# Max-pool and subtract: tiles of six rows in four buffers, without ScalarE and in program order

## The chip, the cores and the metric

The kernel runs on one core of one Trainium2 chip. The metric is the device time of one execution in microseconds (us), given as the median of several runs; less is better.

## The reference

```python
def reference(x):                      # x: (8, 64, 256, 256) float32
    x_r = x.reshape(B, C, oH, 8, oW, 8)
    pooled = x_r.max(axis=(3, 5))
    upsampled = np.repeat(np.repeat(pooled, 8, axis=2), 8, axis=3)
    return (x - upsampled).astype(np.float32)
```

Each 8 x 8 window of each image is reduced to its maximum, and that maximum is subtracted from every element of the window. The input has 134.2 MB and the output as much; every element is read once and written once.

## The kernel before

Eight image lines of 256 floats, which hold 32 whole windows side by side, make one "row" of 2048 floats (8 KB). There are 16384 rows. A tile has 128 partitions with R = 2 consecutive rows in each, so 16 KB per partition and 2 MB in all, and the loop runs over 64 tiles. For each tile:

- L42: SP (SyncE) issues the load of the tile into `dat`, from a pool of 8 buffers.
- L49: VectorE takes the maximum over each window of one row, seen as (32 windows, 8 lines, 8 columns), into `pooled` (32 values). One instruction per row, two per tile.
- L56: ScalarE copies `pooled` into `rep`, each value eight times in a row, so that `rep` has a full line of 256 values for each row. One ACTIVATE per tile, for both rows.
- L64: VectorE subtracts `rep` from `dat` in place; the line of `rep` is read again for each of the eight lines. One instruction per row.
- L74: ScalarE's queue issues the store of `dat` to the output.

The order on each engine isn't the order of the program text: a scheduler places the instructions. On VectorE it has grouped them, three to five reduces of several tiles and then four to six subtracts, and on ScalarE's queue it has put up to three ACTIVATEs ahead of the stores. A load into a buffer waits until the store that last used the buffer has landed. All loads go through SP's queue in order, all stores through ScalarE's queue in order; both queues are served by the same 16 DMA engines.

Of the kernel before, what the change touches and what calls it, by code (L numbers as in the profile page):

```python
# [1 line left out]

# [4 lines left out]


@with_exitstack  # L10
def kernel(
    ctx: ExitStack,
    tc: tile.TileContext,
    x: bass.AP,
    out: bass.AP,
):
    nc = tc.nc
    P = nc.NUM_PARTITIONS

    B, C, H, W = x.shape  # L20
    pH = pW = 8
    oH, oW = H // pH, W // pW

    x_rows = x.rearrange("b c (oh ph) w -> (b c oh) (ph w)", ph=pH)
    out_rows = out.rearrange("b c (oh ph) w -> (b c oh) (ph w)", ph=pH)
    n_rows = x_rows.shape[0]
    row_len = x_rows.shape[1]

    R = 2
    rows_per_tile = P * R  # L30
    ntiles = n_rows // rows_per_tile
    assert n_rows % rows_per_tile == 0

    data_pool = ctx.enter_context(tc.tile_pool(name="data_pool", bufs=8))
    small_pool = ctx.enter_context(tc.tile_pool(name="small_pool", bufs=4))

    for i in range(ntiles):
        dat = data_pool.tile([P, R, row_len], mybir.dt.float32, name="dat")
        src = x_rows[i * rows_per_tile : (i + 1) * rows_per_tile].rearrange(
            "(p r) d -> p (r d)", r=R  # L40
        )
        nc.sync.dma_start(out=dat.rearrange("p r d -> p (r d)"), in_=src)  # L42

        pooled = small_pool.tile([P, R, oW], mybir.dt.float32, name="pooled")
        rep = small_pool.tile([P, R, W], mybir.dt.float32, name="rep")

        for r in range(R):
            in_v = dat[:, r].rearrange("p (ph ow pw) -> p ow ph pw", ph=pH, ow=oW, pw=pW)
            nc.vector.tensor_reduce(  # L49
                out=pooled[:, r],  # L50
                in_=in_v,
                axis=mybir.AxisListType.XY,
                op=mybir.AluOpType.max,
            )

        nc.scalar.activation(  # L56
            out=rep.rearrange("p r (ow pw) -> p (r ow) pw", pw=pW),
            in_=pooled.rearrange("p r ow -> p (r ow)").to_broadcast([P, R * oW, pW]),
            func=mybir.ActivationFunctionType.Copy,
        )  # L60

        for r in range(R):
            dat_v = dat[:, r].rearrange("p (ph w) -> p ph w", ph=pH)
            nc.vector.tensor_tensor(  # L64
                out=dat_v,
                in0=dat_v,
                in1=rep[:, r].unsqueeze(1).to_broadcast([P, pH, W]),
                op=mybir.AluOpType.subtract,
            )

        dst = out_rows[i * rows_per_tile : (i + 1) * rows_per_tile].rearrange(
            "(p r) d -> p (r d)", r=R
        )
        nc.scalar.dma_start(out=dst, in_=dat.rearrange("p r d -> p (r d)"))  # L74


# [1 line left out]
_INS = ['x']  # L78
_OUTS = [((8, 64, 256, 256), 'float32')]


# [23 lines left out]
```

## Time and profile before

| | |
|---|---|
| median of 5 runs | 631.89 us (630.63 to 632.32) |
| the profiled execution: its own time | 632.32 us |
| its span, first to last instruction | 630.3 us |
| VectorE busy | 564.8 us (90%), 256 instructions |
| ScalarE busy | 39.5 us (6%) |
| data moved by the DMA engines | 268.48 MB, mean 426 GB/s |
| load, issue to landing, shortest / median | 7.8 / 30.0 us |
| store, issue to landing, shortest / median | 6.3 / 18.8 us |

A profile is taken from one execution; the span leaves out what lies before the first and after the last instruction. "Busy" of an engine is the time in which it ran instructions. An engine that is busy 90% of the span isn't yet the one that sets the time: what counts is which wait ends last in each stretch. The page cuts the span into 40 slices and gives for each the busy share of the engines in tenths, and the GB/s that the DMA engines moved. A group of instructions is shown with its busy time and the mean duration of one, then with the idle time of the engine just before them and what ended it. "Issue to landing" of a DMA is the time from its issue until its semaphore tells that all its data has arrived.

### The profile page before, as it was taken

The page shows a single profiled execution, that of the slowest core. Times are in us where ns is not written, and L with a number is a line of the kernel's source. Part 1 is how long each engine was busy: PE and PEld are TensorE (multiplying, and loading weights), DVE is VectorE, ACT ScalarE, POOL GpSimd, SP SyncE. Part 2 cuts the span into 40 slices and gives each one's busy share as a digit, 9 for nine tenths or more (in the row PEclk, how much of TensorE's full clock was granted, in tenths as well). Part 3 has the DMA queues.
Part 4 walks back from the last instruction along what each step waited for, and adds up shares of the span by engine and source line. Part 5 has one row for each costly group of instructions (what it writes and reads, how often), then busy time and mean ns, then how long its engine had stood idle before and what let it go on. Part 6 is the DMA issues. An engine that isn't in the chain of part 4 may idle for free.

```text
span 630.3 us, 730 instructions
## 1 busy us (share of the span) xinstructions
DVE 564.8 (90%) x256; ACT 39.5 (6%) x65; POOL 0.2 (0%) x4
## 2 busy tenths in 40 slices
DVE  4999999889889889889889898898998988988985
ACT  1000010010000000000001001001001001001000
POOL 0000000000000000000000000000000000000000
DMA  9999999999999999999999999999999999999997
GB/s 362 417 432 431 426 432 431 431 430 433 432 432 432 433 432 432 430 429 429 431 432 430 433 432 430 433 433 432 432 430 430 429 428 432 430 433 432 433 409 335
DMA packets 18437, 268.48 MB, mean 426 GB/s; under 512 B 2048, under 2 KB 2048, under 8 KB 2048
## 3 DMA queue, kind: packets, MB, share of 16 engines
q1 hardware_dynamic: 9216, 134.22, 50.0%
q10 hardware_dynamic: 9216, 134.22, 49.8%
q14 instruction: 5, 0.04, 0.0%
HBM read 134.22 MB, written 134.22 MB: 426 GB/s over the span
## 4 chain that ended last, share of the span: by engine, by line
DMA 83%; DVE 15%; issue 1%; DVEq 0%; ACT 0%; SPq 0%; ACTq 0%
DMA dat<-in_x_dram 50%; DMA out_dram<-dat 33%; DVE dat L64 9%; DVE pooled L49 6%; DVEq L100 0%; ACT rep L56 0%; SPq L42 0%; ACTq L74 0%; DVEq L64 0%; ACTq L56 0%
## 5 line engine op out<-in xcount | busy, mean ns | idle before, releaser
L49 DVE TENSOR_REDUCE pooled<-dat 128x32 f32<-128x2048 f32 x128 | 285.1, 2278 | 57.6 <-DMA dat<-in_x_dram 57.6
L64 DVE TENSOR_TENSOR dat<-dat,rep 128x2048 f32<-128x2048 f32 x128 | 284.0, 2284 | 0.8 <-ACT rep L56 0.8
L56 ACT ACTIVATE rep<-pooled 128x512 f32<-128x512 f32 x64 | 38.2, 624 | 578.4 <-DMA dat<-in_x_dram 408.1
L56 ACT ACT_TABLE_LOAD x1 | 1.3, 1283 | 0.7 <-PEq L89 0.7
L89 POOL MEMSET const-bfloat16-1.0<- 128x1 bf16 x1 | 0.1, 102 | 0.0
L89 POOL MEMSET const-uint8-127<- 128x1 uint8 x1 | 0.1, 102 | 0.0
L89 POOL MEMSET const-float32-0.0<- 128x1 f32 x1 | 0.1, 99 | 0.2 <-issue 0.2
L89 POOL MEMSET const-float32-1.0<- 128x1 f32 x1 | 0.1, 99 | 0.0
## 6 DMA issues: line engine op xcount, KB each, us to landing
dat<-in_x_dram SPq DMA_DIRECT2D x64, 2048.0 KB, 30.0
out_dram<-dat ACTq DMA_DIRECT2D x64, 2048.0 KB, 18.8
```

The costliest lines, as they stand in the source:

```text
L49: nc.vector.tensor_reduce(out=pooled[:, r], in_=in_v, axis=mybir.AxisListType.XY, op=mybir.AluOpType.max,)
L56: nc.scalar.activation(out=rep.rearrange("p r (ow pw) -> p (r ow) pw", pw=pW), in_=pooled.rearrange("p r ow -> p (r ow)").to_broadcast([P, ...
L64: nc.vector.tensor_tensor(out=dat_v, in0=dat_v, in1=rep[:, r].unsqueeze(1).to_broadcast([P, pH, W]), op=mybir.AluOpType.subtract,)
L89: nc = _bacc.Bacc("TRN2", target_bir_lowering=False, num_devices=1)
```

## The change

The tile has up to six rows per partition (48 KB, 6 MB in all), and there are 25 tiles of different sizes: one of two rows, twenty of six, two of two, two of one. The pool has 4 buffers, each with room for six rows, also where a tile needs fewer. One reduce takes the maxima of all rows of a tile (for a one-row tile there is a form of its own). ScalarE computes nothing and has no table to load: the subtract reads `pooled` directly, each value eight times in a row for each of the eight lines. The subtract stays one instruction per row. The scheduler is switched off with `manual_schedule`, so each engine runs its instructions in the order of the text: the reduce of a tile, its subtracts, then the next tile. Each first subtract waits on VectorE's own semaphore for the reduce ahead of it. Stores stay on ScalarE's queue, loads on SP's.

```diff
+F32 = mybir.dt.float32
+ROW = 2048
+CHUNKS = [2] + [6] * 20 + [2, 2, 1, 1]
...
-    R = 2
-    rows_per_tile = P * R
-    ntiles = n_rows // rows_per_tile
...
+    big = max(CHUNKS)
-    data_pool = ctx.enter_context(tc.tile_pool(name="data_pool", bufs=8))
-    small_pool = ctx.enter_context(tc.tile_pool(name="small_pool", bufs=4))
+    data = ctx.enter_context(tc.tile_pool(name="data", bufs=4))
+    small = ctx.enter_context(tc.tile_pool(name="small", bufs=4))
+    ctx.enter_context(tc.manual_schedule())
+    at = 0
+    for R in CHUNKS:
+        src = x_rows[at : at + P * R].rearrange("(p r) d -> p (r d)", r=R)
+        dst = out_rows[at : at + P * R].rearrange("(p r) d -> p (r d)", r=R)
+        at += P * R
+        dat = data.tile([P, big * ROW], F32, name="dat")[:, : R * ROW]
+        pooled = small.tile([P, big * oW], F32, name="pooled")[:, : R * oW]
+        nc.sync.dma_start(out=dat, in_=src)
-        for r in range(R):
-            in_v = dat[:, r].rearrange("p (ph ow pw) -> p ow ph pw", ph=pH, ow=oW, pw=pW)
+        wins = dat.rearrange("p (r ph ow pw) -> p r ph ow pw", r=R, ph=pH, ow=oW)
+        tops = pooled.rearrange("p (r ow) -> p r ow", r=R)
+        if R == 1:
             nc.vector.tensor_reduce(
-                out=pooled[:, r],
-                in_=in_v,
+                out=tops[:, 0],
+                in_=wins[:, 0].rearrange("p ph ow pw -> p ow ph pw"),
                 axis=mybir.AxisListType.XY,
                 op=mybir.AluOpType.max,
             )
-        nc.scalar.activation(
-            out=rep.rearrange("p r (ow pw) -> p (r ow) pw", pw=pW),
-            in_=pooled.rearrange("p r ow -> p (r ow)").to_broadcast([P, R * oW, pW]),
-            func=mybir.ActivationFunctionType.Copy,
-        )
+        else:
+            nc.vector.tensor_reduce(
+                out=tops,
+                in_=wins.rearrange("p r ph ow pw -> p r ow ph pw"),
+                axis=mybir.AxisListType.XY,
+                op=mybir.AluOpType.max,
+            )
         for r in range(R):
             nc.vector.tensor_tensor(
-                out=dat_v,
-                in0=dat_v,
-                in1=rep[:, r].unsqueeze(1).to_broadcast([P, pH, W]),
+                out=wins[:, r],
+                in0=wins[:, r],
+                in1=tops[:, r].unsqueeze(1).unsqueeze(3).to_broadcast([P, pH, oW, pW]),
                 op=mybir.AluOpType.subtract,
             )
-        nc.scalar.dma_start(out=dst, in_=dat.rearrange("p r d -> p (r d)"))
+        nc.scalar.dma_start(out=dst, in_=dat)
```

In the new text the load is at L44, the reduce at L56 (L49 for one row), the subtract at L63 and the store at L69.

More of the change, by code (lines that the diff above doesn't have):

```diff
@@ L21 @@
     pH = pW = 8
-    oH, oW = H // pH, W // pW
+    oW = W // pW
     x_rows = x.rearrange("b c (oh ph) w -> (b c oh) (ph w)", ph=pH)
     out_rows = out.rearrange("b c (oh ph) w -> (b c oh) (ph w)", ph=pH)
-    n_rows = x_rows.shape[0]
-    row_len = x_rows.shape[1]
-    R = 2
-    rows_per_tile = P * R
-    ntiles = n_rows // rows_per_tile
-    assert n_rows % rows_per_tile == 0
-    data_pool = ctx.enter_context(tc.tile_pool(name="data_pool", bufs=8))
-    small_pool = ctx.enter_context(tc.tile_pool(name="small_pool", bufs=4))
[L37 to L40, printed above, removed]
-        )
-        nc.sync.dma_start(out=dat.rearrange("p r d -> p (r d)"), in_=src)
-        pooled = small_pool.tile([P, R, oW], mybir.dt.float32, name="pooled")
-        rep = small_pool.tile([P, R, W], mybir.dt.float32, name="rep")
-        for r in range(R):
-            in_v = dat[:, r].rearrange("p (ph ow pw) -> p ow ph pw", ph=pH, ow=oW, pw=pW)
+    assert sum(CHUNKS) * P == x_rows.shape[0]
+    big = max(CHUNKS)
[13 more added lines that the diff above has]
+        if R == 1:
             nc.vector.tensor_reduce(
-                out=pooled[:, r],
-                in_=in_v,
+                out=tops[:, 0],
+                in_=wins[:, 0].rearrange("p ph ow pw -> p ow ph pw"),
                 axis=mybir.AxisListType.XY,
@@ L54 @@
             )
-        nc.scalar.activation(
-            out=rep.rearrange("p r (ow pw) -> p (r ow) pw", pw=pW),
-            in_=pooled.rearrange("p r ow -> p (r ow)").to_broadcast([P, R * oW, pW]),
-            func=mybir.ActivationFunctionType.Copy,
-        )
+        else:
[5 more added lines that the diff above has]
+            )
         for r in range(R):
-            dat_v = dat[:, r].rearrange("p (ph w) -> p ph w", ph=pH)
             nc.vector.tensor_tensor(
-                out=dat_v,
-                in0=dat_v,
-                in1=rep[:, r].unsqueeze(1).to_broadcast([P, pH, W]),
+                out=wins[:, r],
+                in0=wins[:, r],
+                in1=tops[:, r].unsqueeze(1).unsqueeze(3).to_broadcast([P, pH, oW, pW]),
                 op=mybir.AluOpType.subtract,
             )
[L71 to L74, printed above, removed]
+        nc.scalar.dma_start(out=dst, in_=dat)
 _INS = ['x']
```

## The prediction

> **What bounds the kernel now.** I read the page from the top: the share of each engine, then the slices, then the queues, and only then the chain, because at 90% VectorE looks like the limit and the slices say otherwise.
>
> ```profile
> DVE 564.8 (90%) x256; ACT 39.5 (6%) x65; POOL 0.2 (0%) x4
> DMA  9999999999999999999999999999999999999997
> GB/s 362 417 432 431 426 432 431 431 430 433 432 432 432 433 432 432 430 429 429 431 432 430 433 432 430 433 433 432 432 430 430 429 428 432 430 433 432 433 409 335
> q1 hardware_dynamic: 9216, 134.22, 50.0%
> q10 hardware_dynamic: 9216, 134.22, 49.8%
> L49 DVE TENSOR_REDUCE pooled<-dat 128x32 f32<-128x2048 f32 x128 | 285.1, 2278 | 57.6 <-DMA dat<-in_x_dram 57.6
> L64 DVE TENSOR_TENSOR dat<-dat,rep 128x2048 f32<-128x2048 f32 x128 | 284.0, 2284 | 0.8 <-ACT rep L56 0.8
> L56 ACT ACTIVATE rep<-pooled 128x512 f32<-128x512 f32 x64 | 38.2, 624 | 578.4 <-DMA dat<-in_x_dram 408.1
> ```
>
> The load queue (q1) and the store queue (q10) together fill 99.8% of the DMA engines' time, at 428 to 433 GB/s in nearly all slices. VectorE's 57.6 us of idle time are all waits for loads. So the transfers set the pace: 268.44 MB (the two queues) at the 431.3 GB/s of the windows from 100 to 500 us are 622.4 us, of a span of 630.3. The kernel loses only 7.9 us. The change can win some of that, or alter the rate. The window table finds the lost time at the two ends.
>
> ```profile
> 0.00:2.00 2.00, 0.00 (x0) 1.28 (x1) 0.20 (x4) 1.00 0.48 90
> 2.00:3.00 1.00, 0.00 (x0) 0.01 (x1) 0.00 (x0) 1.00 0.62 147
> 3.00:4.00 1.00, 0.00 (x0) 0.00 (x0) 0.00 (x0) 1.00 0.79 311
> ...
> 610.00:615.00 5.00, 5.00 (x3) 0.00 (x0) 0.00 (x0) 1.00 0.86 364
> 615.00:620.00 5.00, 4.25 (x3) 0.63 (x1) 0.00 (x0) 1.00 0.99 423
> ...
> 622.00:623.00 1.00, 1.00 (x1) 0.00 (x0) 0.00 (x0) 1.00 0.09 33
> 623.00:624.00 1.00, 0.15 (x1) 0.00 (x0) 0.00 (x0) 1.00 0.00 0
> 624.00:625.00 1.00, 0.00 (x0) 0.00 (x0) 0.00 (x0) 1.00 1.23 524
> ```
>
> The last two columns are the DMA engines' busy share and GB/s. The first 4 us move 0.64 MB, worth 1.5 us: 2.5 us lost. From 4 to 32 us another 0.6 goes. From 610 on, 6.85 MB (15.9 us' worth) take 20.3: 4.4 us lost, namely 0.8 in 610 to 615, 2.2 in 615 to 624, and 1.4 around the last store. The sum, 7.5, agrees with the 7.9 but for rounding. The cause is in the timeline of the end:
>
> ```profile
> 611.33 4.74 ACTq L74 DMA_DIRECT2D out_dram<-dat  x2
> 615.62 2.28 DVE L49 TENSOR_REDUCE pooled<-dat 128x32 f32<-128x2048 f32 x1
> 618.00 0.63 ACT L56 ACTIVATE rep<-pooled 128x512 f32<-128x512 f32 x1 [15.45 <-DVE pooled L49]
> 618.66 4.49 DVE L64 TENSOR_TENSOR dat<-dat,rep 128x2048 f32<-128x2048 f32 x2 [0.76 <-ACT rep L56]
> 623.18 0.34 ACTq L74 DMA_DIRECT2D out_dram<-dat  x1
> ```
>
> The last store is issued 7.1 us after the one ahead of it, and 2 MB last only 4.86 us: the engines run dry and wait for VectorE.
>
> **The change, part by part.** One row (128 x 2048 floats, 1.049 MB) is 2.431 us of transfer each way.
>
> *ScalarE and VectorE.* The 64 ACTIVATEs (39.5 us with the table load) go. ScalarE waits 578 us in all and VectorE waited for it once (0.76 us), so nearly nothing is gained but that 0.76, which lies in the tail. VectorE's instructions start 2.20 us apart (4.40 for two in the chain). A six-row tile costs 13.2 for its subtracts and at most 13.2 for the reduce; what one reduce in place of six saves I leave out. Held to program order, the first subtract now waits for the reduce of its own tile: between 0 and the 0.8 us that the trip through ScalarE took; I take 0.2, since there is no second engine in it. That makes 26.6 us per tile, 27.2 at worst, beside 12 rows of transfer = 29.2. Nothing else is queued on VectorE that could use the wait; the store behind it is late by the same 0.2. The cover is the 2.6 us by which VectorE is faster.
>
> *The subtract's new operand*, each pooled value read eight times in a row, is in no row for VectorE. Below: 2.20 us, as L49, which reads pieces of eight floats, costs what the contiguous L64 does (2278 and 2284 ns). Above: ScalarE does such a read at L56 in 624 ns for 512 results; were all of that per element, 2048 would take 2.50. I take 2.20, the same engine. VectorE becomes the bound at (29.2 - 13.2 - 0.2)/6 = 2.63, above both ends, so this costs nothing here.
>
> *Four buffers of six rows for eight of two.* A buffer comes round every 4 x 29.2 = 116.7 us. It needs 29.2 for the load at half rate, 2.95 around it (7.8 us shortest landing less 4.86), 26.6 on VectorE, 29.2 and 1.45 (6.3 less 4.86) for the store: 89.4. 27 us are spare (before: 77.8 less 32.6 = 45). On SP's queue each load waits for the store four tiles earlier, and all later loads stand behind it; while it waits, up to 27 us of stores stand ready, so the engines stay filled. Cost 0; without that cover about 3 us per tile.
>
> *Start.* The first load stays two rows, so the 2.5 us stay, and I keep the 0.6. The second tile lands near 25.5 us (issued at 0.73 with the first, eight rows 19.4, 2.95 around, 2.4 for the first store's share), so VectorE idles from 17.5 to 25.5 where it had worked. The first big store is issued near 52. Until then the queue holds 26 rows of loads and a two-row store, 68 us: covered, cost 0.
>
> *The end.* Small tiles still occupy whole buffers, so the last one-row load waits for the store of the last six-row tile. In the window table the last store of before, issued at 623.18, moves from 624.0: 0.8 of the 1.45 lie ahead of the data, 0.65 behind. So from the six-row store's last byte the last row needs 0.65 to be seen, 2.95 and 4.86 (one row at half rate) to land, 4.6 on VectorE, 0.8 until its store moves: 13.9 us. The cover is five rows of stores and this load's row, 14.6. So 0.7 us to spare; landings here varied, so the gap is 0 to 2, and I take 0.5. With the 1.4 around the last store the end loses 1.9 in place of 4.4: -2.5.
>
> *Packets.* 64 DMAs each way become 25; at 144 packets each (9216/64) there are 7200 where there were 18432, most three times as long. What a packet costs of itself no view shows. From the slices: 429 GB/s would be +3.3 us, 433 would be -2.4; a gain of twice the step from 431 to 433, to 435, would be -5.3. Fewer packets speak for a gain, the filled engines for a small one: -1.0.
>
> The Trainium skill weighs in twice. Its page "SBUF — State Buffer", section "The DMA setup-cost knee", gives each transfer a fixed 2 us: with 78 DMAs fewer that would be an estimated -156 us. The 99.8% of this trace refute it for a kernel with several DMAs in flight. "DMA: Bandwidth & Descriptors", section "Why small descriptors are slow", names some 3 cycles of overhead per packet on a 32-byte bus; estimated from that, 16 KB pays 3 in 515 and 48 KB 3 in 1539, together -2.4 us, and the sum would be 1.4 lower.
>
> **Sum:** 630.3 - 2.5 - 1.0 = 626.8 of span; the execution's time was 632.32, 2.0 more than its span: 628.8. That execution lies 0.4 above the median of 631.89, so for the median 628.4.
>
> **Rivals.** A measurement of this kernel can tell about 0.2%, 1.3 us.
>
> *A much better rate.* If packets are the whole reason for 431, 435 GB/s gives 624.1; from 433 on, below 627. For it: three times fewer packets. Against: 99.8% busy leaves no gap in sight.
>
> *No change.* The end gives its gain back: with the last landings 2 to 4 us later than the shortest ones I used, the one-row load comes too late for its cover. 630.6 to 633. For it: only 0.7 us to spare, and a median load landing of 30 us. Against: the queues are nearly empty by then.
>
> *Slower: VectorE becomes the bound.* Its place is L63 with the new operand, its point 2.63 us per row. At 3.0: 8.6 for the first landing, 128 x 5.2, 25 x 0.2 and 4.7 for the last one-row store (7.1 less 2.4) = 684 of span, 686. For it: 90% busy now, and an operand that no row shows. Against: both bounds lie below the point. The rate falling under 429 with coarse packets also ends on this side, near 633 to 635.
>
> **How the numbers follow.** Forecast (ends better, rate 431 to 433) 0.54; much better rate 0.17; no change 0.14; slower 0.15 (half VectorE, half rate). Faster is 0.54 + 0.17 = 0.71. The range goes from 624, the 435 end, to 633, the end of the no-change case; outside lie the slow cases and little else.
>
> **What would show it.** The subtract's mean near 2284 ns and one reduce of six rows under 13.7 us; VectorE idle before reduces, waiting for loads; slices at 431 to 433 throughout; no empty window before the last store. The forecast is wrong if the reduce never waits for a load after the first few tiles, if a middle slice lies below 428, or if over 2 us without traffic precede the last store.

## The result, and the profile after

The changed kernel takes 633.9 us (median of 22 runs, 631.64 to 640.76), the kernel before 631.86 (42 runs, 630.63 to 632.42). The ratio is 1.0039, with a 95% interval of 1.0028 to 1.0051: slower by 0.4%, where 0.5% faster was forecast. The runs also lie much further apart than those of before. The profiled execution took 635.32 us, with a span of 633.5 (before: 632.32 and 630.3). A run more than 1.5% above the fastest of the same kernel counts as slow; the medians and ranges of experiments 1, 4, 8 and 9 include such runs.

The page of the changed kernel, first the engines and the slices, then the queues and VectorE's two large groups:

```profile
DVE 560.3 (88%) x153; POOL 0.2 (0%) x4
DMA  9999999999999999999999999999999999999994
GB/s 381 427 425 422 447 444 410 438 438 444 410 444 438 441 413 441 441 441 413 441 444 428 422 444 444 422 428 444 441 413 441 438 444 413 441 417 431 447 389 165
q1 hardware_dynamic: 3600, 134.22, 49.3%
q10 hardware_dynamic: 3600, 134.22, 49.1%
L56 DVE TENSOR_REDUCE pooled<-dat 128x192 f32<-128x12288 f32 (+1 forms) x23 | 272.3, 11838 | 56.0 <-DMA dat<-in_x_dram 56.0
L63 DVE TENSOR_TENSOR dat<-dat,pooled 128x2048 f32<-128x2048 f32 x128 | 284.1, 2286 | 0.9
```

VectorE is as before: busy a little less, waiting for loads. The subtract costs what it did (2286 ns, before 2284). The transfers again fill the span. Two things differ: the middle slices are higher in the mean (with packets of 1.8 us a slice catches more or fewer of them, hence 410 beside 444), and the last slice falls to 165. The window tables of the changed kernel, with one line of the kernel before ahead of them (the last two columns are the DMA engines' busy share and GB/s):

```profile
100.00:500.00 400.00, 363.37 (x166) 23.52 (x40) 0.00 (x0) 1.00 1.01 431
...
100.00:500.00 400.00, 371.87 (x101) 0.00 (x0) 1.00 1.00 434
560.00:600.00 40.00, 33.11 (x11) 0.00 (x0) 1.00 1.01 433
600.00:615.00 15.00, 8.33 (x4) 0.00 (x0) 1.00 0.95 398
615.00:622.00 7.00, 4.10 (x2) 0.00 (x0) 1.00 0.76 315
622.00:629.00 7.00, 4.58 (x2) 0.00 (x0) 1.00 0.14 59
629.00:633.50 4.50, 0.00 (x0) 0.00 (x0) 1.00 0.57 233
```

The middle runs at 433.8 GB/s (mean of the four windows of 100 us), before at 431.3: 618.9 us of data in place of 622.4, a gain of 3.5. From 600 on the DMA engines lose 11.3 us (each window's length less its GB/s share of 433.8: 1.2 + 1.9 + 6.0 + 2.1), where the end of before lost 4.4: 6.9 more. The two make +3.4; the span grew by 3.2. So the middle got better, and the end gave back twice as much. VectorE's timeline shows what the end waited for:

```profile
583.18 4.41 DVE L56 TENSOR_REDUCE pooled<-dat 128x64 f32<-128x4096 f32 x1
598.94 4.42 DVE L56 TENSOR_REDUCE pooled<-dat 128x64 f32<-128x4096 f32 x1 [6.82 <-DMA dat<-in_x_dram]
614.52 2.29 DVE L49 TENSOR_REDUCE pooled<-dat 128x32 f32<-128x2048 f32 x1 [6.63 <-DMA dat<-in_x_dram]
624.17 2.29 DVE L49 TENSOR_REDUCE pooled<-dat 128x32 f32<-128x2048 f32 x1 [5.04 <-DMA dat<-in_x_dram]
626.49 2.29 DVE L63 TENSOR_TENSOR dat<-dat,pooled 128x2048 f32<-128x2048 f32 x1
```

Three of the four small tiles make VectorE wait 5 to 7 us, 18.5 in all: their loads come late. The last two of them have one row each.

### The profile page after: what moved, and what is told of

Its sections match the earlier page's. It is cut to its first block, busy times and chain, and to the rows that moved or that the text cites. A ratio compares the mean times of both kernels' runs of the same rounds, so it can differ in the third digit from the quotient of the medians.

```text
span 633.5 us, 315 instructions
## 1 busy us (share of the span) xinstructions
DVE 560.3 (88%) x153; POOL 0.2 (0%) x4
## 4 chain that ended last, share of the span: by engine, by line
another core or an unknown queue 45%; DVE 29%; DMA 23%; issue 1%; SPq 1%
DVE pooled L56 14%; DVE dat L63 14%; DMA out_dram<-dat 12%; DMA dat<-in_x_dram 11%; SPq L44 1%; DVE pooled L49 0%
## 5 line engine op out<-in xcount | busy, mean ns | idle before, releaser
L56 DVE TENSOR_REDUCE pooled<-dat 128x192 f32<-128x12288 f32 (+1 forms) x23 | 272.3, 11838 | 56.0 <-DMA dat<-in_x_dram 56.0
L63 DVE TENSOR_TENSOR dat<-dat,pooled 128x2048 f32<-128x2048 f32 x128 | 284.1, 2286 | 0.9
L49 DVE TENSOR_REDUCE pooled<-dat 128x32 f32<-128x2048 f32 x2 | 4.6, 2286 | 11.7 <-DMA dat<-in_x_dram 11.7
## 6 DMA issues: line engine op xcount, KB each, us to landing
dat<-in_x_dram SPq DMA_DIRECT2D x3, 2048.0 KB, 26.2
```

The costliest lines, as they stand in the source:

```text
L49: nc.vector.tensor_reduce(out=tops[:, 0], in_=wins[:, 0].rearrange("p ph ow pw -> p ow ph pw"), axis=mybir.AxisListType.XY, op=mybir.AluOp ...
L56: nc.vector.tensor_reduce(out=tops, in_=wins.rearrange("p r ph ow pw -> p r ow ph pw"), axis=mybir.AxisListType.XY, op=mybir.AluOpType.max,)
L63: nc.vector.tensor_tensor(out=wins[:, r], in0=wins[:, r], in1=tops[:, r].unsqueeze(1).unsqueeze(3).to_broadcast([P, pH, oW, pW]), op=mybir ...
```

## The experiments

Each was compared with the kernel before on the same chip, whose median stayed between 631.72 and 631.83 us.

**1. One buffer for the small tiles.** The first suspicion was the chain of buffers: each small load waits for the store of one of the last big tiles.

```diff
+TAIL = 4
...
+    for n, R in enumerate(CHUNKS):
...
+        if n < len(CHUNKS) - TAIL:
             dat = data.tile([P, big * ROW], F32, name="dat")[:, : R * ROW]
+        else:
+            if tail_at == 0:
+                last = data.tile([P, big * ROW], F32, name="dat")
+            dat = last[:, tail_at * ROW : (tail_at + R) * ROW]
+            tail_at += R
```

> The four small tiles at the end share one six-row buffer, so their loads wait only for the store four big tiles back and not, one after the other, for the stores of the last four big tiles. Theory A (the loss sits in this chain: the last one-row load was issued at 612.6 us, when the slowest DMA engine had finished the last six-row store, and the DMA engines ran dry for some 7 us): the last loads are issued near 550 us, no dry stretch is left before the last store, span 619 (data at 434 GB/s) + 2.5 + 0.6 + 1.4 at the last store + 2 to 3 for the slowest engine = 625 to 627, time 627 to 629, and the runs lie closer together than 632 to 641. Theory B (one DMA engine is late by itself, whatever waits for it): the end gains 2 us at most, time 631 to 633, and the wide spread stays. Theory C (a six-row store so near the end is what costs): about as after, 633 to 635.

Measured: 632.35 us (628.77 to 638.7), ratio 1.0001 (0.9982 to 1.002). Theory A fell: all four small loads were issued by 555.3 us, as meant, and the last one came hardly earlier for it (623.3 us; in the changed kernel 624.2). VectorE's timeline of this kernel, whose brackets again name the wait for the load:

```profile
600.70 4.42 DVE L64 TENSOR_REDUCE pooled<-dat 128x64 f32<-128x4096 f32 x1 [5.27 <-DMA dat<-in_x_dram]
616.02 2.29 DVE L57 TENSOR_REDUCE pooled<-dat 128x32 f32<-128x2048 f32 x1 [6.38 <-DMA dat<-in_x_dram]
623.35 2.29 DVE L57 TENSOR_REDUCE pooled<-dat 128x32 f32<-128x2048 f32 x1 [2.71 <-DMA dat<-in_x_dram]
```

A load of 1 MB that is issued at 555 and lands at 623 isn't waiting for a buffer. The result alone would fit theory B. The records of the single DMA packets in the two traces say something else. These are packets started in 4 us, on all 16 engines, of the load and of the store queue:

```
changed kernel       load 16 KB   store 48 KB
576 to 580 us            26            32
580 to 584               30            23
584 to 588               31            24
588 to 592               34            24
one buffer for tail  load  8 KB   store 48 KB
600 to 604 us            29            32
```

The two queues get about the same number of packets, not of bytes. The order shows it too. Strung together so that each packet starts where another ends, to within 0.08 us, the packets of 576 to 592 us form 16 chains, one for each engine, and in 222 of 224 steps along them the two queues take turns. One of the chains (L is a load's packet, S a store's, and s one of 4 bytes, of which each transfer has one for each engine):

```
LSLSLSLSLsLSLSLS
```

That is theory D of the next runs, and its sums come near the landings. A packet's recorded duration is 309 ns for 8 KB, 611 for 16 and 1815 for 48, and each engine has 8 packets of a load. The changed kernel's two-row load issued at 572.7 needs 8 x (611 + 1815) = 19.4 us beside six-row stores, and with 2.95 around it 22.4; it took 26.2. The one-row load issued at 594.1 needs 8 x (309 + 1815) + 2.95 = 19.9; it took 20.4. The last, beside two-row stores, 8 x (309 + 611) + 2.95 = 10.3; it took 11.6. Sharing by bytes would give 12.7, 7.8 and 7.8. These are the landings of the slowest of the 16 engines, for which VectorE has to wait; on the median engine, whose stores were done earlier, the three loads were there after 21.5, 14.6 and 5.4 us.

**2. Two-row tiles in program order.** The changed kernel with its tiles and buffers as before: program order and the directly read operand alone.

```diff
-CHUNKS = [2] + [6] * 20 + [2, 2, 1, 1]
+CHUNKS = [2] * 64
-    data = ctx.enter_context(tc.tile_pool(name="data", bufs=4))
+    data = ctx.enter_context(tc.tile_pool(name="data", bufs=8))
```

> Program order and the directly read operand alone: 64 tiles of two rows in eight buffers, as before. Theory A with the packet price (6 ns for each packet of 16 KB and its share of the semaphore packets): the middle stays at 431 GB/s, 622.4 us of data; in program order the last load (landed near 604.6 us) is worked off by 614, so the end no longer runs dry: span 622.4 + 2.5 + 0.6 + 1.4 = 627, time 629, 3 us faster than before. Rival (the rate rises with the new instructions or the missing ScalarE, not with the packets): middle at 433 to 434, time 625 to 626. Rival (order is worth nothing): 631 to 632, as before.

Measured: 630.58 us (630.28 to 630.83), ratio 0.9979 (0.997 to 0.9987). Its middle and its end, by windows:

```profile
100.00:500.00 400.00, 372.91 (x127) 0.00 (x0) 1.00 1.01 431
600.00:622.00 22.00, 12.44 (x5) 0.00 (x0) 1.00 1.01 431
622.00:628.80 6.80, 0.00 (x0) 0.00 (x0) 1.00 0.58 248
```

The rate is that of before, so it came with the six-row tiles and not with the new instructions. The traffic no longer breaks off ahead of the last store, as expected. The gain is 1.3 us, not 3: the 16 shares of the last store, one for each DMA engine, land over 1.9 us, and the end waits for the slowest engine.

**3. Without the small tiles at the end.**

```diff
-CHUNKS = [2] + [6] * 20 + [2, 2, 1, 1]
+CHUNKS = [2] + [6] * 21
```

> The small tiles at the end are taken away, 21 tiles of six rows after the first of two. Theory A: the last load waits for the store four tiles back alone and lands near 586 us; VectorE needs 26.3 until 612.5; the store 0.8 + 14.5 + 0.65: span near 629, time 630 to 632, though the DMA engines then stand idle for over 10 us before the last store, where they have nothing to do. That would say that the small tiles at the end bring nothing as they are buffered. Rival (small tiles shorten the end as meant, and something else in the middle costs): a whole six-row tile of VectorE and store stands open at the end, 26 + 15 us less the 16 that the small tiles had, time 645 to 655.

Measured: 630.2 us (629.32 to 632.95), ratio 0.9986 (0.9974 to 0.9999), 3.7 us less than with the small tiles. The last load landed by 585.13 (586 expected), and the stretch ahead of the last store is thin, but nothing is late:

```profile
600.00:613.00 13.00, 11.41 (x6) 0.00 (x0) 1.00 0.72 310
613.00:628.40 15.40, 0.00 (x0) 0.00 (x0) 1.00 0.83 357
```

So the small tiles, buffered as they are, cost more than they bring.

**4. The scheduler on again.**

```diff
-    ctx.enter_context(tc.manual_schedule())
```

> The changed kernel with the scheduler on again, which puts the reduces of two tiles ahead of their subtracts. Theory A (the end's chain of buffers sets the time, not the order on VectorE): the store of the first of two tiles is late by 13 us, of 27 us that a buffer has to spare, so the middle stays at 433 to 434 GB/s and VectorE's order changes the end by a few us: time 632 to 641, as the changed kernel's own runs lie. Rival (program order is what keeps the loads coming): each pair of tiles loses some us to waits of the loads, VectorE waits over 100 us in all, time over 645.

Measured: 650.49 us (645.74 to 663.58), ratio 1.0242 (1.0218 to 1.0266). The rival's time held in every run, and its reason nearly: VectorE waited 99 us for loads, and the middle fell to 386 to 415 GB/s. These figures and the timeline are of the longest execution, 663.58 us, and need not be those of the others. The order on VectorE:

```profile
154.96 12.94 DVE L55 TENSOR_REDUCE pooled<-dat 128x192 f32<-128x12288 f32 x1
179.32 12.95 DVE L55 TENSOR_REDUCE pooled<-dat 128x192 f32<-128x12288 f32 x1 [11.42 <-DMA dat<-in_x_dram]
192.19 24.30 DVE L62 TENSOR_TENSOR dat<-dat,pooled 128x2048 f32<-128x2048 f32 x11
```

My expectation had left out a wait: with two reduces ahead, the subtracts of a tile that is ready at 167.9 wait until the next tile has landed (179.3) and been reduced (192.2). The first tile's store is late by 24 us here, not by 13, of some 25 that a buffer has to spare (experiment 8). With four buffers the scheduler's order costs 2.4%.

**5. The last tile in parts.** The test of theory D: against experiment 1 only the four small loads become one. The lines shown are against the changed kernel.

```diff
+CHUNKS = [2] + [6] * 21
+PARTS = [(0, 2), (2, 4), (4, 5), (5, 6)]
...
         nc.sync.dma_start(out=dat, in_=src)
...
+        for r0, r1 in PARTS if at == x_rows.shape[0] else [(0, R)]:
...
+            nc.scalar.dma_start(out=dst[:, part], in_=dat[:, part])
```

> The last six rows come as one load of 48 KB packets; VectorE and the stores take them in the parts of two, two, one and one rows. Against the kernel with one buffer for the tail only the four small loads are made one. Theory D (the DMA engines take turns between the two queues by packets, not by bytes: from 576 to 592 us of the changed kernel's trace 121 load packets of 16 KB went beside 103 store packets of 48 KB, so a small load got a quarter, and a one-row load a seventh, of an engine while six-row stores were queued, and the last rows came late): the last load lands near 586 us, VectorE works without a wait until 612, the stores never run dry for long, span 619 + 2.5 + 0.6 + 1.4 + 1 to 2 for the slowest engine = 625, time 626 to 628, runs within 3 us. Theory B (one DMA engine late by itself): 630 to 632 with a wide spread, as with one buffer for the tail. Theory C (big stores near the end): no change against 632.

Measured: 627.33 us (626.07 to 630.12), ratio 0.9932 (0.9917 to 0.9947). It beats both kernels, and it is 5.0 us less than experiment 1. The runs lie 4 us apart, not within 3. In its timeline the same six rows are there by 587.5, and VectorE doesn't wait again:

```profile
587.50 4.42 DVE L60 TENSOR_REDUCE pooled<-dat 128x64 f32<-128x4096 f32 x1 [3.08 <-DMA dat<-in_x_dram]
596.37 4.41 DVE L60 TENSOR_REDUCE pooled<-dat 128x64 f32<-128x4096 f32 x1
605.22 2.28 DVE L53 TENSOR_REDUCE pooled<-dat 128x32 f32<-128x2048 f32 x1
609.75 2.28 DVE L53 TENSOR_REDUCE pooled<-dat 128x32 f32<-128x2048 f32 x1
```

**6. The same, with small packets in the last load.** The suspected cost put back by itself: same bytes, buffers, waits and number of instructions (the output is spread likewise).

```diff
+        last = at + P * R == x_rows.shape[0]
+        how = "(r p) d -> p r d" if last else "(p r) d -> p (r d)"
-        src = x_rows[at : at + P * R].rearrange("(p r) d -> p (r d)", r=R)
-        dst = out_rows[at : at + P * R].rearrange("(p r) d -> p (r d)", r=R)
+        src = x_rows[at : at + P * R].rearrange(how, r=R)
+        dst = out_rows[at : at + P * R].rearrange(how, r=R)
...
```

> As the kernel with the last tile in parts, but that tile's rows are spread so that its one load has packets of 8 KB in place of 48 KB (the same bytes, buffers, waits and instructions). Theory D: while the stores of the three tiles ahead of it (43.7 us of data) are queued, the load gets 309 of 309 + 1815 ns on each engine, so about half of its 14.5 us of data is done when they end near 600, and it lands at 605 to 612 in place of 586; VectorE needs 26 after that, span 640 to 646, time 642 to 648. Theory B or any sharing by bytes: the load lands near 586 as before, the smaller packets cost under 0.5 us, time within 1 us of the kernel with the last tile in parts.

Measured: 644.18 us (643.4 to 644.3), ratio 1.0191 (1.0178 to 1.0204), 17 us more than experiment 5. The wait is where theory D put it:

```profile
609.99 4.42 DVE L63 TENSOR_REDUCE pooled<-dat 128x64 f32<-128x4096 f32 x1 [29.01 <-DMA dat<-in_x_dram]
```

The load landed at 610.0, inside the 605 to 612 of theory D and 22 us after its twin with large packets. Here a queue's share of an engine went by packets. That small packets as such make a load late is ruled out by experiment 7: there the same load, in the same 8 KB packets but beside stores of 8 KB, has landed by 589.6.

**7. All packets of 8 KB.** Experiment 5, with every tile spread as in 6, so all packets are equal.

```diff
-        src = x_rows[at : at + P * R].rearrange("(p r) d -> p (r d)", r=R)
+        src = x_rows[at : at + P * R].rearrange("(r p) d -> p r d", r=R)
...
```

> As the kernel with the last tile in parts, but every load and store in packets of 8 KB, all sizes equal. Packet price (611 ns for 16 KB and 1815 for 48 KB in the packets' durations; middle rates of 431.3 and 433.8 GB/s: about 5 ns for each packet beside 27.2 bytes per ns): 8 KB take 306.4 ns, middle at 428 GB/s, 627.5 us of data, 8 to 9 us more than with 48 KB: time 634 to 637. Theory D says besides that the end is as short as with equal packets of 48 KB, the last load landing near one quarter to half a tile's time after its turn. Rival (the rate comes from the six-row tiles, not from packets): middle at 433 to 434 and the time of the kernel with the last tile in parts.

Measured: 634.24 us (634.13 to 634.45), ratio 1.0037 (1.0025 to 1.0049). Its middle, and VectorE's wait for its last load:

```profile
100.00:500.00 400.00, 371.33 (x100) 0.00 (x0) 1.00 1.01 428
...
589.57 4.42 DVE L61 TENSOR_REDUCE pooled<-dat 128x64 f32<-128x4096 f32 x1 [3.10 <-DMA dat<-in_x_dram]
```

428 GB/s as expected. With 431 at 16 KB and 434 at 48 KB the rate follows the packet's size, not the tile's; experiment 10 adds six-row tiles in 16 KB packets, at 432. And the runs lie within 0.3 us of each other.

**8. Three buffers.** Experiment 5 with one buffer less.

```diff
-    data = ctx.enter_context(tc.tile_pool(name="data", bufs=4))
+    data = ctx.enter_context(tc.tile_pool(name="data", bufs=3))
```

> As the kernel with the last tile in parts, with three buffers in place of four. By the prediction's step on buffers a tile's round needs 29.0 + 2.95 + 26.2 + 29.0 + 1.45 = 88.6 us and three tiles of transfer give 87.0: 0.5 us lost per tile, 11 over the run, less where a transfer has the engines alone and runs faster than half rate: time 628 to 640, and VectorE waits longer before each reduce. Rival (the step on buffers was wrong and four are already too few, as one DMA engine lags): over 650.

Measured: 658.38 us (652.51 to 672.63), ratio 1.0418 (1.036 to 1.0477): over the 640 of the prediction's step, and within the rival's "over 650". The profiled execution is the shortest, 652.51 us. A whole round can be read from its chain of waits (start, us, what):

```profile
226.15 31.50 DMA dat<-in_x_dram
...
257.67 12.97 DVE pooled L60
...
270.66 13.31 DVE dat L67 x6
...
283.99 32.64 DMA out_dram<-dat
```

31.5 + 26.3 + 32.6 with the gaps are 90.6 us, not 88.6: the store takes 2 more. For three tiles that is 30.2 each in place of 29.0, 24 us over twenty tiles, of the 25 that this execution lost against experiment 5. Why two of the four runs took 10 and 20 us more is not shown. The rival had the time but not the reason: with four buffers, in experiment 5, the middle keeps 434 GB/s. The step on buffers is right in kind and 2 us low in a round; four buffers (4 x 29.0) have some 25 us to spare.

**9. Four-row tiles in six buffers.** Experiment 5 with 32 tiles of four rows, the last in parts of two, one and one.

```diff
-CHUNKS = [2] + [6] * 21
-PARTS = [(0, 2), (2, 4), (4, 5), (5, 6)]
+CHUNKS = [4] * 32
+PARTS = [(0, 2), (2, 3), (3, 4)]
...
-    data = ctx.enter_context(tc.tile_pool(name="data", bufs=4))
-    small = ctx.enter_context(tc.tile_pool(name="small", bufs=4))
+    data = ctx.enter_context(tc.tile_pool(name="data", bufs=6))
+    small = ctx.enter_context(tc.tile_pool(name="small", bufs=6))
```

> As the kernel with the last tile in parts, with 32 tiles of four rows in six buffers (the same 24 rows in all, packets of 32 KB), the last tile in parts of two, one and one rows. Packet price: (1204 + 5) ns for 32 KB, middle at 433.4, 0.6 us more data time than with 48 KB. If the lag of the slowest DMA engine grows with the packets' size (landings of one transfer spread over 0.9 us with 8 KB, 1.9 with 16 KB, 2.5 to 5 with 48 KB), it is 2 to 3 us here and the runs lie closer together: time 626 to 628, about equal to the kernel with the last tile in parts. If the lag is chance alone, the spread of times stays at 4 us. If four-row tiles give up the rate: 630.

Measured: 633.69 us (631.96 to 644.34), ratio 1.0037 (1.0016 to 1.0059). The middle runs at 433 GB/s as expected, but the lag and the spread were not. In the profiled execution the shares of its last parts' stores landed over 5.9 us, at least two of the 16 some 5 us after the median. Without the three longest runs the times still lie from 631.96 to 639.53. The profiled execution with its lag is the fastest of them, so a lag of this size isn't what sets the slower ones apart.

**10. Six-row tiles with 16 KB packets.** Experiment 5 with a six-row tile made of three blocks of two rows; the last tile in three parts of two.

```diff
-        src = x_rows[at : at + P * R].rearrange("(p r) d -> p (r d)", r=R)
+        src = x_rows[at : at + P * R].rearrange("(c p r) d -> p c (r d)", r=2, p=P)
...
```

> As the kernel with the last tile in parts, but every packet of 16 KB (a six-row tile is made of three blocks of two rows), the last tile in three parts of two rows. It parts two readings of the slowest DMA engine's lag (0.9 us at the end with 8 KB packets, 1.9 in the kernel of two-row tiles, 5.0 and 5.9 with 48 and 32 KB). If the packets' size makes the lag: 1 to 2.5 us here, runs within 1 us of each other, span 622.4 + 2.5 + 0.6 + 1.4 + 2 = 629, time 630 to 631. If the 24 rows in flight make it (two-row tiles had 16): 4 to 6 us and runs spread over 4 us, median 632 to 635. Packet price in both: middle at 431 GB/s.

Measured: 629.36 us (629.14 to 629.51), ratio 0.9964 (0.995 to 0.9977). The rate:

```profile
100.00:500.00 400.00, 372.82 (x101) 0.00 (x0) 1.00 1.01 432
```

The last store's shares land within 0.8 us. So 24 rows in flight alone don't make the lag; packets of 32 and 48 KB went with a large one (5.9 and 5.0 us at the end of their profiled executions) and 8 and 16 KB with a smaller one (0.9, and 0.8 to 2.3). But 32 KB had a larger one than 48, and experiment 3 with 48 KB had 2.5 near its end, so packet size isn't shown to be all of it. Why one or a few engines fall behind in some executions stays open.

## Why the prediction was wrong

**The bound.** Right: the transfers set the pace, the loss lies at the ends, VectorE is covered.

**ScalarE, VectorE, the operand.** Right. The subtract kept its 2.29 us; the six-row reduce took 12.95 (at most 13.2 was assumed); the subtract began 0.04 after it (0.2 taken). 26.2 us per tile for the predicted 26.6.

**Four buffers and the start.** Right. The second tile landed at 24.3 (25.5 predicted), and the traffic from 4 to 40 us was that of before (426 GB/s, before 425); in the steady part VectorE waited 2.2 to 3.2 us for each load. Experiment 8 puts the spare time at some 25 us for the 27.

**Packets.** Right in sign, mis-sized: -1.0 was taken of a range from +3.3 to -5.3, and -3.5 measured. The filled queues hid it: 99.8% busy counts a packet's own overhead as busy. The durations show it: 16 KB to 48 KB adds 1204 ns, 301 for each 8 KB, and the 309, 611 and 1815 ns lie 8 to 9 above that, a fixed part of each packet. The rates give an estimate of 5 to 6 ns (3.5 us of 16 engines over 9984 data packets fewer). The Trainium skill's page "DMA: Bandwidth & Descriptors", section "Why small descriptors are slow", whose 3 cycles came to an estimated 2.4 us in the prediction, was nearer than I was.

**The end.** This step failed, and it made the result. It read: "2.95 and 4.86 (one row at half rate) to land", against a cover of "five rows of stores and this load's row". Half rate holds only for packets of equal size. In the trace of before the packets of both queues have 16 KB, so sharing by packets and by bytes look the same there, and I carried the half over to loads of 16 and 8 KB packets beside stores of 48 KB. They get a quarter and a seventh; the last load, on the slowest engine, gets a third beside packets of 16 KB. The small loads landed after 26.2, 20.4 and 11.6 us, where the prediction's way of counting gives 12.7, 7.8 and 7.8. The cover came late with them: the last of its five rows of stores was issued at 619.2 us, after the load that it was to cover (612.6). Experiment 5 takes the small packets out of the loads and wins 6.6 us against the changed kernel; experiment 6 puts small ones back and loses 17. Experiment 1 shows that the buffers, the prediction's own worry, were by themselves worth some 1.5 us, within the scatter of its runs.

The same page of the skill, section "Queues, rings and completion order", says that each engine goes round its queues packet by packet. The traces agree as to turns by packet (121 to 103 in 16 us, in turns in 222 of 224 steps); the 9 to 17 descriptors that it gives for a typical packet don't show here, where one contiguous run of 16 or 48 KB was one turn. Applied to the diff with one run as one packet, that rule would have come near the landings above.

A second part of the step was too simple: "landed" was one moment for 16 engines. These are the landings of the 16 shares of three transfers of the changed kernel, in us:

```
                                  first   median   last
load of the last six-row tile     553.5   553.7    557.0
store of the last six-row tile    604.0   604.2    612.5
last one-row load                 617.7   617.9    624.1
```

The last load is issued when the last share has landed, 8.3 us after the median engine was done; meanwhile the other engines use up the two-row stores that were to be the cover. From 622 to 629 there is hardly traffic (59 GB/s), though the last store is still to come. In this execution the late issue, 8.3 us, weighs more than the slow landing, 11.6 us in place of 7.8. No run takes the lag away by itself, so what each part cost the median isn't shown; with the last loads issued early, in experiments 1 and 5, the small packets alone are worth some 5 us. That the times scatter would fit a slowest engine that stands in the chain twice, but each kernel has a trace of one execution only.

**The rivals and the signs.** "No change" named the right place, the one-row load too late for its cover, and a landing 2 to 4 us later than counted, as it was (3.8); the packets and the late issue aren't in it, and its 630.6 to 633 end just short of 633.9. "A much better rate" had the right middle, 433.8 for its "from 433 on"; experiment 5, with this middle and another end, took 627.3, close to its "below 627". VectorE never came near its point of 2.63 us per row. The sign "over 2 us without traffic" before the last store all but came (59 GB/s for 7 us). The sign "a middle slice lies below 428" came as well, but was ill chosen: slices of 410 belong to a middle of 434 in the mean. One reading was off without weight: the last store of before was issued 7.4 us after the one ahead of it (615.74 and 623.18), not 7.1.

## What to carry to other kernels

Where two DMA queues are full, count how large the packets (contiguous runs) of each are: in these runs a queue with small packets beside one with large packets got the smaller share, so small tiles at the end that were meant to shorten the tail arrived late. Load the last tile like all others, and split only its compute and its stores. A rate or a share read from a trace in which all packets are equal doesn't hold for a change that makes them unequal.

## What was not expected of the hardware

A transfer's share of a DMA engine went by the number of packets: the same 6 MB load landed at 587.5 us with packets of 48 KB and at 610.0 with packets of 8 KB. The rate with equal packets rose from 428 GB/s at 8 KB over 431 at 16 to 434 at 48. And the 16 engines drift apart: the shares of one transfer landed over at most 2.8 us in the traces with packets of 8 or 16 KB alone, and over 5 to 7 us in some with 32 or 48 KB (up to 21 in experiment 1, which has both). The times of the kernels with small packets also agree better (634.13 to 634.45 us for experiment 7, 631.96 to 639.53 for nine of the twelve runs of experiment 9); that the drift is the reason isn't shown.
